# The next-to-last expert of a mixture also finishes its own rows on chip

## The chip, the cores and the metric

The kernel runs on one core of one Trainium2 chip. The metric is the device time of one launch in microseconds (us): the median of several runs. The profile is of one execution; its times count from the start of its span.

## The reference

One encoder layer over 2048 tokens of 1024 features: neighbourhood attention and a spatial gating unit share an input and an output projection, a layer norm follows, and then a mixture of experts with a second layer norm. The change touches only the mixture. Each token picks one of 4 groups of experts, and two of the 4 experts in it:

```python
def hierarchical_moe(h, w_rg, b_rg, w_re, b_re, w_gate, w_up, w_down):
    ...
    y = jnp.zeros_like(hf)
    for e in range(MOE_EXPERTS):
        act = jax.nn.silu(hf @ w_gate[e]) * (hf @ w_up[e])
        y = y + combine[:, e:e + 1] * (act @ w_down[e])
    return y.reshape(B, T, D)
...
x = layer_norm(DEEPNORM_ALPHA * x + moe_out, ln2_g[l], ln2_b[l])
```

`combine` is zero but for a token's two experts. The kernel divides the last line by ALPHA: it adds the weighted expert outputs to the first norm's result and normalizes that with a suitably smaller epsilon.

## The kernel before, in words

Routing sorts the tokens. `table` holds a list of rows for each expert (token number to gather, token number to add to, weight), `gtok` one for each group. The first norm's result lies in DRAM twice: `x1d`, which experts gather from, and `xad`, to which their outputs are added.

The experts are worked through as 18 jobs (`JOBS`, lines 36 and 37), ordered so that the four experts of a group follow each other and the largest come first. A job has up to 384 rows in parts of at most 128; jobs 14 to 17 are the last group's four experts, job 16 has two parts of 128 rows, job 17 parts of 128 and 64. In `main` (line 1313) the loop of line 1626 goes over the jobs j, and in it u = 0 to 3 counts four units. In unit u TensorE (PE) multiplies a quarter of job j's gate and up weights (`gate_up`, line 1164). Beside that, the unit issues work for neighbouring jobs: `listed` (1121) loads job j+2's list, `gather` (1135) fetches its rows into one of four buffers `xg`, `flip` (1144) transposes job j+1's rows, `load_gu` and `load_d` (1069, 1099) load weights by SyncE's (SP's) DMA queue, and `down` (1227) multiplies a part of job j-1 by its down weights, scales it on ScalarE (ACT) into a tile `y`, and adds that to `xad` with an indirect DMA of GpSimd (POOL), `add_rows` (1253). Most products are split into high and low halves, three matmuls each; job 17 (`G32`, `D32`) uses plain fp32.

When a group's last job has been added, its tokens are finished in tiles of 128 (`GTILES`: 6, 5, 5, 3). `records` (1539) loads the group's list. `combine` (1488) is a generator that goes one step further in each unit: it fetches a tile from `xad`, lets three units pass (`WAIT`), then issues the statistics and the first instruction of the norm, in the next unit the second, in the next the place, an indirect DMA to `out`. `CU` and `CT` say in which units a new tile joins: `CT` = (0, 2) in jobs 15 to 17. A tile's norm costs VectorE (DVE) `bn_stats` twice and `bn_aggr`, POOL two small instructions (line 1453 and the power in `inv`, 1456), and DVE two instructions over 128x1024, `first` (1461) and `second` (1464):

```python
        def combine(g, rec):
            x = fetch(g, rec)
            for _ in range(WAIT):
                yield
            yield from norm(x)
            place(x, rec)
            yield pipe
```

The last group is finished by `last` (1509), which follows a string, `TAIL` (63). Its tiles 0 to 2 come from the group's list; its tiles 3 and 4 are job 17's own two parts. Those rows' sum before job 17 is fetched into the `xg` buffers that the gathered rows have left, and job 17's output is added on chip, by DVE from PSUM. The letters are: f fetch, d down product and addition, s statistics on DVE, a statistics on ACT (`act_stats`, 1496), c `first`, v `second`, o place. The fetches are issued in unit 2 of job 17, everything else after its unit 3. Tokens of job 17 stand in the group's list too, so their place ("fin") waits until the places of tiles 0 to 2 ("out") have landed.

PE, ACT, DVE and POOL take their instructions in the order in which the program issues them; nothing reorders them. `apart` (1239) says which DMAs on `xad` must wait for which: a fetch of a group waits for the adds of the group's latest job.

Of the kernel before, what the change touches and what calls it, by code (L numbers as in the profile page):

```python
# [8 lines left out]
F32 = mybir.dt.float32  # L9
# [3 lines left out]
OP = mybir.AluOpType  # L13
# [45 lines left out]
D32 = (17,)  # L59
DN = 0, 0  # L60
TU = 3
CT = (0, 2)
TAIL = "f0 f3 f1 f4 f2", "s0 c0 d3 a1 v0 d4 o0 c1 a2 v1 o1 c2 a3 v2 o2 a4 c3 v3 o3 c4 v4 o4"
AW1 = 3
# [947 lines left out]
class Moe:  # L1012
    def __init__(self, c, w_gate, w_up, w_down, ln2g, ln2b, out):
        self.c, self.es = c, ExitStack()
        self.w = w_gate, w_up, w_down
        self.ln2g, self.ln2b, self.out = ln2g, ln2b, out
        self.gw, self.dw, self.ex = {}, {}, []
        self.xt, self.act, self.idx, self.added = {}, {}, {}, [[], [], [], []]
        self.parts, self.slot, n = [], [], 0
        for _, lo, hi in JOBS:  # L1020
            self.parts.append([min(P, hi - lo - o) for o in range(0, hi - lo, P)])
            self.slot.append(n)
            n += len(self.parts[-1])
# [97 lines left out]
    def listed(self, j):  # L1121
# [10 lines left out]
        if m:  # L1132
            nc.sync.dma_start(t[0:m, n], c.table[bass.ds(base + (lo + n * P), m), :])

# [78 lines left out]
    def products(self, j, s):  # L1213
        ah, al = self.acts[2 * (j % 2):2 * (j % 2) + 2]
        o = slice(s * P, s * P + self.parts[j][s])
        for n in range(2):
            po = self.bank("gu" if j in D32 else "yp")[0:self.parts[j][s], :]
# [9 lines left out]
    def down(self, j, s):  # L1227
        c, tc, nc = self.c, self.c.tc, self.c.nc
        m = self.parts[j][s]
        y = self.sp.tile([P, D], F32, name="y")  # L1230
        w = self.idx[j][0:m, s, 2:3].bitcast(F32)
# [4 lines left out]
        tc.add_to_no_dep_group(f"add{j}", r.ins)  # L1236
        self.apart(r, JOBS[j][0] // 4, j)

    def apart(self, r, g, add=None):
# [73 lines left out]
    def main(self):  # L1313
# [160 lines left out]
        def fetch(g, rec, x=None):  # L1474
# [3 lines left out]
                                         bounds_check=T, oob_is_err=False)  # L1478
            self.apart(r, g)
            return x  # L1480

# [26 lines left out]

        def last(n):
            j = nj - 1  # L1510
            x = [None] * n + [xg[(self.slot[j] + s) % NXG][0:m, :] for s, m in enumerate(self.parts[j])]
            rows = [recs[3][:, i] for i in range(n)] + [self.idx[j][0:m, s] for s, m in enumerate(self.parts[j])]
            z, mean, r, sums = {}, {}, {}, {}
            for ops in TAIL:
                for op, i in ((o[0], int(o[1])) for o in ops.split()):
                    if op == "f":
                        x[i] = z[i] = fetch(3, rows[i], x[i])
                    elif op == "d":
                        su = sums[i] = small(x[i], "csu", 5)
                        for h, po in self.products(j, i - n):  # L1520
                            hs = slice(h * 512, (h + 1) * 512)
                            V.scalar_tensor_tensor(x[i][:, hs], po, rows[i][:, 2:3].bitcast(F32), x[i][:, hs],
                                                   op0=OP.mult, op1=OP.add, accum_out=su[:, 3 + h:4 + h])
                        z[i] = xp.tile([P, D], F32, name="y")[0:self.parts[j][i - n], :]
                    elif op == "s":
                        m, r[i] = stats(x[i])
                        mean[i] = m, OP.subtract
                    elif op == "a":
                        m, r[i] = act_stats(x[i], sums.get(i))
                        mean[i] = m, OP.add  # L1530
                    elif op == "c":
                        first(z[i], x[i], *mean[i])
                    elif op == "v":
                        second(z[i], r[i])
                    elif op == "o":
                        place(z[i], rows[i], out, "out" if i < n else "fin")
                yield

# [82 lines left out]
        nj = len(JOBS)  # L1621
        todo, recs = [], {}
        junk = pl.tile([P, D], F32, name="junk")
        self.load_d(pipe, 2, 0, LAG)
        self.load_gu(pipe, 3, 0, LAG)
        for j in range(2, nj):
# [4 lines left out]
            for u in range(4):  # L1631
# [20 lines left out]
                if f < 2 and jn < nj:  # L1652
                    self.load_d(pipe, jn, f, LAG)
                if j in LASTS and u == 2:
                    recs[LASTS[j]] = records(LASTS[j])
                if j < nj - 1 and j - 1 in LASTS and u == (TU if j == nj - 4 else 3):
                    todo += [(LASTS[j - 1], i) for i in range(GTILES[LASTS[j - 1]])]
                pipe.step()
                if todo and u in (CU if j < nj - 3 else CT):
                    g, i = todo.pop(0)  # L1660
                    pipe.add(combine(g, recs[g][:, i]))
                if j == nj - 1 and u >= 2:
                    if u == 2:
                        tail = last(GTILES[3])
                    else:
                        pipe.flush()
                        assert not todo
                    next(tail)
        for _ in tail:
            pass  # L1670
        rare()
# [76 lines left out]
```

## Time and profile before

| | us |
|---|---|
| median of 3 runs (lowest, highest) | 1306.78 (1304.14, 1308.53) |
| the profiled execution, its own time | 1304.38 |
| its span in the profile | 1302.7 |
| PE busy | 1229.2 |
| DVE busy | 763.6 |
| ACT busy | 569.1 |
| POOL busy | 404.3 |

In a timeline a row is an instruction, or several alike in a row: start and duration in us, the engine, the line of the kernel, the operation, the tiles written and read (`cx` is a tile being finished, `xg` a gathered part, `crec` and `ix` are lists, `cr` and `csu` small numbers of a norm), shapes, how many, and in brackets how long the engine stood idle before it and what ended that. SPq is the DMA queue of SP. A DMA's row is its issue, not its transfer.

### The profile page before, as it was taken

What the parts mean: (1) busy time and instruction counts of PE and PEld (TensorE: products, weight loads), DVE (VectorE), ACT (ScalarE), POOL (GpSimd) and SP (SyncE); (2) the same over time, 40 slices, a digit from 0 to 9 for tenths busy, and PEclk for the clock granted to TensorE, in tenths of its full rate; (3) what the DMA queues carried; (4) which work ended last, traced back from release to release, by engine and by line L of the source; (5) the groups of instructions that cost most, each with busy time, mean ns of one, the idle gap of its engine ahead of it and who ended that gap; (6) DMA issues with size and microseconds to landing.
All of it is one profiled execution on the core that took longest, in us unless ns stands there. A gap on an engine that the chain in (4) does not pass through costs nothing. (4 is left out here: it accounts for less than half of the span.)

```text
span 1302.7 us, 22220 instructions
## 1 busy us (share of the span) xinstructions
PE 1229.2 (94%) x7948; PEld 1048.2 (80%) x7948; DVE 763.6 (59%) x1647; ACT 569.1 (44%) x1202; POOL 404.3 (31%) x416
## 2 busy tenths in 40 slices
PE   9999999999999898999999999988898999999980
PEld 7888888888888687888888888768787899989970
DVE  5366233426733226675675776866466578778665
ACT  5243142323331247554454545334556555655522
POOL 0011000001100013333534434432223357566575
PEclk9999999999999898999999999999899999999995
DMA  8514434541257669678578676362999899999984
GB/s 258 186 49 162 162 129 164 183 171 33 98 186 239 201 204 271 179 210 195 141 210 193 156 210 193 112 216 83 252 285 294 247 275 322 301 271 317 301 243 136
DMA packets 136161, 261.72 MB, mean 201 GB/s; under 512 B 51120, under 2 KB 60592, under 8 KB 136048
## 3 DMA queue, kind: packets, MB, share of 16 engines
q1 hardware_dynamic: 118064, 204.88, 50.0%
q0 software_dynamic: 17984, 55.40, 15.6%
q8 instruction: 63, 1.03, 0.3%
q14 instruction: 50, 0.41, 0.1%
HBM read 184.17 MB, written 80.24 MB: 203 GB/s over the span
## 5 line engine op out<-in xcount | busy, mean ns | idle before, releaser
L142 DVE TENSOR_TENSOR wl<-wr,wh 128x512 fp32r<-128x512 f32 (+1 forms) x132 | 125.5, 963 | 112.4 <-ACT wh L141 101.4
L653 POOL TENSOR_SCALAR lg<-lg,s 128x352 f32<-128x352 f32 (+3 forms) x128 | 79.6, 622 | 291.2 <-DVE s L652 231.9
L141 ACT CAST wh<-wr 128x512 fp32r<-128x512 f32 (+1 forms) x132 | 109.0, 839 | 87.7 <-DMA wr<-w_in 37.3
L131 PE MATMUL acc<-wh,xh 128*128 128x512 f32 x320 | 125.8, 393 | 0.4 <-ACT wh L141 0.4
L133 PE MATMUL acc<-wh,xl 128*128 128x512 f32 x320 | 124.7, 390 | 0.0
L132 PE MATMUL acc<-wl,xh 128*128 128x512 f32 x320 | 124.7, 390 | 0.0
L131 PE MATMUL gu<-xh,wh 128*128 128x256 f32 (+2 forms) x416 | 124.0, 298 | 0.0
L133 PE MATMUL gu<-xh,wl 128*128 128x256 f32 (+2 forms) x416 | 123.6, 297 | 0.0
L132 PE MATMUL gu<-xl,wh 128*128 128x256 f32 (+2 forms) x416 | 123.5, 297 | 0.0
L668 ACT COPY pT<-pt 128x384 f32<-128x384 f32 (+3 forms) x128 | 57.5, 449 | 109.9 <-PE pt L666 109.1
L131 PE MATMUL acc<-xh,wh 128*128 128x512 f32 x256 | 100.4, 392 | 0.0
L133 PE MATMUL acc<-xh,wl 128*128 128x512 f32 x256 | 99.7, 389 | 0.0
L132 PE MATMUL acc<-xl,wh 128*128 128x512 f32 x256 | 99.6, 389 | 0.0
L640 DVE CUSTOM_DVE_ANT_0 lg<-l,tm 128x352 f32<-128x352 f32 (+3 forms) x128 | 57.8, 452 | 69.2 <-PE l L133 55.8
L271 POOL TENSOR_TENSOR r<-va,mhalf 128x32 f32<-128x32 f32 x4 | 22.4, 5612 | 229.2 <-DVE va L269 229.2
L1254 POOL DMA_INDIRECT xad<-y,ix x38 | 64.1, 1687 | 68.1 <-ACT y L1233 46.7
L131 PEld LDWEIGHTS gu<-xh,wh 128*128 128x128 f32 x416 | 78.8, 190 | 1.4
L132 PEld LDWEIGHTS gu<-xl,wh 128*128 128x128 f32 x416 | 78.7, 189 | 1.2
L133 PEld LDWEIGHTS gu<-xh,wl 128*128 128x128 f32 x416 | 78.7, 189 | 0.0
L1139 POOL DMA_INDIRECT xg<-x1d,ix x40 | 48.0, 1201 | 82.8 <-DMA ix<-table 50.4
L133 PEld LDWEIGHTS acc<-wh,xl 128*128 128x128 f32 x320 | 60.1, 188 | 12.9 <-DVE xl L142 0.3
L131 PEld LDWEIGHTS acc<-wh,xh 128*128 128x128 f32 x320 | 60.2, 188 | 12.7 <-ACT wh L141 0.7
(327 smaller groups left out, 3179.7 us busy)
## 6 DMA issues: line engine op xcount, KB each, us to landing
wr<-w_in SPq DMA_DIRECT2D x72, 256.0 KB
wr<-w_down SPq DMA_DIRECT2D x34, 512.0 KB
kt<-kd SPq DMA_DIRECT2D x24, 704.0 KB
wr<-w_gate SPq DMA_DIRECT2D x30, 512.0 KB
wr<-w_up SPq DMA_DIRECT2D x30, 512.0 KB
sd<-kt SPq DMA_DIRECT2D x16, 512.0 KB
qb<-qd SPq DMA_DIRECT2D x64, 128.0 KB
sr<-sd SPq DMA_DIRECT2D x16, 512.0 KB
```

What stands on the lines that cost most here:

```text
L131: nc.tensor.matmul(out, lhsT=ahi, rhs=bhi, start=first, stop=False)
L132: nc.tensor.matmul(out, lhsT=ahi, rhs=blo, start=False, stop=False)
L133: nc.tensor.matmul(out, lhsT=alo, rhs=bhi, start=False, stop=last)
L141: nc.scalar.copy(hi, src)
L142: nc.vector.tensor_tensor(lo, src, hi.bitcast(F32), op=OP.subtract)
L271: nc.gpsimd.tensor_tensor(r, va, mhalf[:, :, :], op=OP.pow)
L640: nc.vector.tensor_tensor_reduce(out=l[:, :N], in0=o.rearrange("p r c -> p (r c)"), in1=bias, scale=-1.0, scalar=3.0e38, op0=OP.add, op1=O ...
L653: nc.gpsimd.tensor_scalar(l[:, :N], l[:, :N], s, 1.0, op0=OP.mult, op1=OP.mult)
L668: nc.scalar.copy(w[0:n, 0:len(ch)], pt[0:n, 0:len(ch)])
L1139: nc.gpsimd.indirect_dma_start(out=self.xg[(self.slot[j] + s) % NXG][0:m, :], out_offset=None, in_=c.x1d[0:rows, :], in_offset=bass.Indire ...
L1254: return self.c.nc.gpsimd.indirect_dma_start(out=self.c.xad[0:rows, :], out_offset=bass.IndirectOffsetOnAxis(ap=ix, axis=0), in_=y, in_off ...
```

## The change

Job 16's parts become the tiles 5 and 6 of `last`. In unit 3 of job 16 five fetches are issued: tiles 0 to 2, and job 16's own rows (5, 6), before job 16's output is in `xad`. The letter e is new: it adds job 16's `y` to its tile on chip. Job 16's output is still added to `xad`, because job 17's rows and the others need it; those two adds now wait for the five fetches (`reads`). `DN` moves job 16's two down products from unit 0 of job 17 to unit 1. Tiles 0 to 2 are finished in the units of job 17; in its unit 3 tiles 3 and 4 are fetched and tiles 5 and 6 finished; behind the loop `ENDS` finishes tiles 3 and 4. Places are now in three classes, "out", "pen" and "fin", each after the one before.

The last group's list is loaded in unit 2 of job 15 rather than job 16. `CT` lets the five tiles of the group before join in units 0 to 3 of job 15 (the first joins in unit 3 of job 14, as before); a tile's fetch is issued in the unit after it joins. So these five are fetched in units 0, 1, 2, 3 of job 15 and 0 of job 16, where it was 0, 1, 3 of job 15 and 1, 3 of job 16.

For job 17's 64-row part the two halves of the output go to partitions 0 to 63 and 64 to 127 of one PSUM bank, and their matmuls alternate between the two column groups of PE. The part's list is loaded twice, so that the weights lie on both halves of the partitions.

```diff
-DN = 0, 0
+DN = 1, 1
-CT = (0, 2)
-TAIL = "f0 f3 f1 f4 f2", "s0 c0 d3 a1 v0 d4 o0 c1 a2 v1 o1 c2 a3 v2 o2 a4 c3 v3 o3 c4 v4 o4"
+CT = (0, 1, 2, 3), (), ()
+TAIL = {(16, 3): "f0 f1 f2 f5 f6", (17, 0): "s0 c0", (17, 1): "v0 o0 s1 c1", (17, 2): "v1 o1 a2 c2 v2 o2",
+        (17, 3): "f3 f4 e5 a5 e6 a6 c5 v5 o5 c6 v6 o6"}
+ENDS = "d3 a3 d4 a4 c3 v3 o3 c4 v4 o4"
+HALF = 64
...
         if m:
-            nc.sync.dma_start(t[0:m, n], c.table[bass.ds(base + (lo + n * P), m), :])
+            for o in (0, HALF) if j in D32 else (0,):
+                nc.sync.dma_start(t[o:o + m, n], c.table[bass.ds(base + (lo + n * P), m), :])
...
+        if j in D32 and self.parts[j][s] == HALF:
+            po = self.bank("gu")
+            for k in range(2):
+                for n in range(2):
+                    self.c.nc.tensor.matmul(po[n * HALF:(n + 1) * HALF, :], lhsT=self.act[j, k][:, o],
+                                            rhs=self.dw[j, k][0][:, n * 512:(n + 1) * 512], start=k == 0, stop=k == 1)
+            for n in range(2):
+                yield n, po[n * HALF:(n + 1) * HALF, :]
+            return
...
         self.apart(r, JOBS[j][0] // 4, j)
+        info = mybir.DependencyInfo(mybir.DependencyClass.Sync, mybir.DependencyReason.DATA)
+        for name in self.reads if j == len(JOBS) - 2 else ():
+            tc.add_manual_dep(r.ins, name, info, reason="read first")
...
             self.apart(r, g)
+            if rec is not None and g == 3:
+                self.reads.append(r.ins.name)
...
+        def last(ops):
+            if ops and not fin:
+                fin.update({i: (None, None, None, recs[3][:, i]) for i in range(GTILES[3])})
+                fin.update(enumerate(own(nj - 1) + own(nj - 2), GTILES[3]))
...
+                elif op == "e":
+                    V.tensor_tensor(x, x, self.ys[j, k][0:x.shape[0], :], op=OP.add)
...
+                elif op == "o":
+                    place(z[i], row, out, {None: "out", nj - 2: "pen", nj - 1: "fin"}[j])
...
-                if j in LASTS and u == 2:
+                if j in LASTS and u == 2 and j < nj - 2:
                     recs[LASTS[j]] = records(LASTS[j])
+                if j == nj - 3 and u == 2:
+                    recs[3] = records(3)
...
-                if todo and u in (CU if j < nj - 3 else CT):
+                if todo and u in (CU if j < nj - 3 else CT[j - nj + 3]):
                     g, i = todo.pop(0)
                     pipe.add(combine(g, recs[g][:, i]))
-                if j == nj - 1 and u >= 2:
-                    if u == 2:
-                        tail = last(GTILES[3])
-                    else:
-                        pipe.flush()
-                        assert not todo
-                    next(tail)
-        for _ in tail:
-            pass
+                if j == nj - 1 and u == 3:
+                    pipe.flush()
+                    assert not todo
+                last(TAIL.get((j, u), ""))
+        last(ENDS)
```

## Rows read from the trace of the kernel before

**Rows 1.** The page: each engine's busy time, share of the span, instructions.

```profile
PE 1229.2 (94%) x7948; PEld 1048.2 (80%) x7948; DVE 763.6 (59%) x1647; ACT 569.1 (44%) x1202; POOL 404.3 (31%) x416
```

**Rows 2.** Busy times by stretch: PE, PEld, DVE, ACT, POOL, TensorE clock, DMA share, GB/s.

```profile
1280.00:1290.00 10.00, 0.00 (x0) 0.00 (x0) 7.72 (x7) 4.85 (x13) 8.80 (x10) 0.50 0.26 104
```

**Rows 3.** Timeline of DVE, jobs 16 and 17: start, duration, instruction, idle before.

```profile
1229.32 1.28 DVE L1450 BATCH_NORM_STATS2 cst<-cx 128x6 f32<-128x512 f32 x2 [2.56 <-DMA cx<-xad,crec]
...
1236.68 1.29 DVE L1450 BATCH_NORM_STATS2 cst<-cx 128x6 f32<-128x512 f32 x2 [1.64 <-DMA cx<-xad,crec]
...
1240.59 0.42 DVE L1207 TENSOR_TENSOR sg<-gu,sg 128x256 f32<-128x256 f32 x1
...
1241.83 1.28 DVE L1465 SCALAR_TENSOR_TENSOR cx<-cx,cr,l2b 128x1024 f32<-128x1024 f32 x1
1244.13 1.23 DVE L142 TENSOR_TENSOR dl<-wr,dh 128x1024 fp32r<-128x1024 f32 x1 [1.02 <-ACT dh L141]
...
1256.63 1.29 DVE L1450 BATCH_NORM_STATS2 cst<-cx 128x6 f32<-128x512 f32 x2 [5.25 <-DMA cx<-xad,crec]
...
1261.41 1.28 DVE L1450 BATCH_NORM_STATS2 cst<-cx 128x6 f32<-128x512 f32 x2
...
1262.97 1.28 DVE L1462 SCALAR_TENSOR_TENSOR cx<-cx,cmv,l2g 128x1024 f32<-128x1024 f32 x1
```

**Rows 4.** Timeline of POOL, from job 16 to the tail's five reads.

```profile
1246.68 1.04 POOL L1476 DMA_INDIRECT cx<-xad,crec  x1 [0.30 <-issue]
...
1253.64 1.60 POOL L1254 DMA_INDIRECT xad<-y,ix  x1 [1.30 <-ACT y L1233]
1255.55 1.58 POOL L1254 DMA_INDIRECT xad<-y,ix  x1 [0.30 <-issue]
...
1265.30 1.94 POOL L1476 DMA_INDIRECT cx<-xad,crec  x1 [0.35 <-issue]
...
1270.17 0.96 POOL L1476 DMA_INDIRECT xg<-xad,ix  x1 [0.30 <-issue]
1271.44 1.01 POOL L1476 DMA_INDIRECT cx<-xad,crec  x1 [0.30 <-issue]
```

**Rows 5.** Timeline of DVE in the tail.

```profile
1270.49 1.29 DVE L1450 BATCH_NORM_STATS2 cst<-cx 128x6 f32<-128x512 f32 x2 [4.22 <-DMA cx<-xad,crec]
...
1277.24 0.74 DVE L1522 SCALAR_TENSOR_TENSOR xg<-gu,ix,xg 64x512 f32<-64x512 f32 x1 [0.80 <-DMA xg<-xad,ix]
...
1284.22 1.28 DVE L1465 SCALAR_TENSOR_TENSOR cx<-cx,cr,l2b 128x1024 f32<-128x1024 f32 x1 [0.74 <-POOL cr L1458]
1285.43 1.28 DVE L1462 SCALAR_TENSOR_TENSOR y<-xg,csu,l2g 128x1024 f32<-128x1024 f32 x1
1287.43 1.28 DVE L1465 SCALAR_TENSOR_TENSOR y<-y,cr,l2b 128x1024 f32<-128x1024 f32 x1 [0.73 <-POOL cr L1458]
...
1290.63 1.28 DVE L1465 SCALAR_TENSOR_TENSOR y<-y,cr,l2b 64x1024 f32<-64x1024 f32 x1 [0.73 <-POOL cr L1458]
```

**Rows 6.** Timeline of POOL at the end.

```profile
1286.51 0.24 POOL L1506 TENSOR_SCALAR csu<-csu 128x1 f32<-128x1 f32 x1
...
1287.63 2.02 POOL L1483 DMA_INDIRECT out<-cx,crec  x1 [0.23 <-issue]
...
1294.49 0.93 POOL L1483 DMA_INDIRECT out<-y,ix  x1 [0.30 <-POOLq L1549]
```

**Rows 7.** Timeline of SP's queue: the last group's list.

```profile
1244.36 0.33 SPq L1544 DMA_DIRECT2D crec<-gtok  x1
```

**Rows 8.** Timeline of ACT in the tail: two tiles' sums.

```profile
1276.31 1.06 ACT L1500 ACTIVATE junk<-cx 128x1024 f32<-128x1024 f32 x1 [16.72 <-DMA cx<-xad,crec]
...
1279.00 1.06 ACT L1500 ACTIVATE junk<-cx 128x1024 f32<-128x1024 f32 x1
```

**Rows 9.** Timeline of PE: job 16's and job 17's down products.

```profile
1248.94 0.50 PE L131 MATMUL yp<-dh,a 128*128 128x512 f32 x1 [1.98 <-ACT a L141]
...
1264.58 8.12 PE L1222 MATMUL gu<-dh,sg 128*128 128x512 f32 x14 [1.90 <-DVE sg L1207]
```

More of the change, by code (lines that the diff above doesn't have):

```diff
@@ L1018, in __init__ @@
         self.xt, self.act, self.idx, self.added = {}, {}, {}, [[], [], [], []]
+        self.ys, self.reads = {}, []
         self.parts, self.slot, n = [], [], 0
@@ L1229, in down @@
         m = self.parts[j][s]
-        y = self.sp.tile([P, D], F32, name="y")
+        y = self.ys[j, s] = self.sp.tile([P, D], F32, name="y")
         w = self.idx[j][0:m, s, 2:3].bitcast(F32)
@@ L1507, in act_stats @@
             return su[:, 1:2], inv(su[:, 2:3])
[L1509 to L1537, printed above, removed]
@@ new lines, in own @@
+        def own(j):
+            return [(j, s, xg[(self.slot[j] + s) % NXG][0:m, :], self.idx[j][0:m, s])
+                    for s, m in enumerate(self.parts[j])]
+        def last(ops):
+            if ops and not fin:
+                fin.update({i: (None, None, None, recs[3][:, i]) for i in range(GTILES[3])})
+                fin.update(enumerate(own(nj - 1) + own(nj - 2), GTILES[3]))
+            for op, i in ((o[0], int(o[1])) for o in ops.split()):
+                j, k, x, row = fin[i]
+                if op == "f":
+                    x = fetch(3, row, x)
+                    fin[i], z[i] = (j, k, x, row), x
+                elif op == "d":
+                    su = sums[i] = small(x, "csu", 5)
+                    for h, po in self.products(j, k):
+                        hs = slice(h * 512, (h + 1) * 512)
+                        o = HALF * h if x.shape[0] == HALF else 0
+                        w = self.idx[j][o:o + x.shape[0], k, 2:3].bitcast(F32)
+                        V.scalar_tensor_tensor(x[:, hs], po, w, x[:, hs], op0=OP.mult, op1=OP.add,
+                                               accum_out=su[:, 3 + h:4 + h])
+                    z[i] = xp.tile([P, D], F32, name="y")[0:x.shape[0], :]
+                elif op == "e":
+                    V.tensor_tensor(x, x, self.ys[j, k][0:x.shape[0], :], op=OP.add)
+                elif op == "s":
+                    m, rstd[i] = stats(x)
+                    mean[i] = m, OP.subtract
+                elif op == "a":
+                    m, rstd[i] = act_stats(x, sums.get(i))
+                    mean[i] = m, OP.add
+                elif op == "c":
+                    first(z[i], x, *mean[i])
+                elif op == "v":
+                    second(z[i], rstd[i])
+                elif op == "o":
+                    place(z[i], row, out, {None: "out", nj - 2: "pen", nj - 1: "fin"}[j])
@@ L1622, in main @@
         todo, recs = [], {}
+        fin, z, mean, rstd, sums = {}, {}, {}, {}, {}
         junk = pl.tile([P, D], F32, name="junk")
```

## The prediction

> **What bounds the kernel now.** I read the page first: TensorE (PE) is busy for 94% of the span, so a microsecond is saved either on PE or behind its last matmul [rows 1]. Next I read the busy times by stretch: from 1280 to 1290 us PE does nothing, VectorE (DVE) is busy for 7.72 of 10 us and GpSimd (POOL) for 8.80, and TensorE is granted 0.50, its 1.2 GHz level [rows 2]. The change moves work in this tail and just ahead of it. The chain of waits has only the last write in it, so I followed the tail by hand in the timelines of DVE and POOL, two engines that take their instructions in the order of the program.
>
> DVE first [rows 3]. While PE works on job 16, DVE waits for rows that finishing tiles of the group before (I call them c0 to c4) have fetched: 2.56 us for c0, 1.64 for c1, 5.25 for c3. So it runs late: c4's statistics, called for in unit 2 of job 17, start at 1261.41. Then POOL [rows 4]: the reads of the last group's three tiles and of job 17's two own parts (f0, f3, f1, f4, f2) stand behind c4's two small POOL instructions and begin at 1265.30. f0's rows are there at 1270.49, when DVE starts on them, f4's at 1277.24 [rows 5]. From then on the tail is a tempo: one tile's second instruction follows the other's after 3.21 us (1284.22, 1287.43, 1290.63), because each waits for two small POOL instructions. It ends with the write issued at 1294.49, over at 1295.42, and 7.28 us follow it to the end of the span [rows 6].
>
> **The change, part by part.** I call the issue of f0 X, and ask where X goes and how long the way is from X to the end. Before it is 1302.7 - 1265.30 = 37.4 us.
>
> *Spacing of c1 to c4 and the earlier list.* c2, c3 and c4 are now read in units 2 and 3 of job 15 and unit 0 of job 16, so c3's 5.25 us wait has no cause any more. X comes behind c4's small instructions in unit 3 of job 16. DVE must do all that stands ahead of it. I start at c1's second instruction, 1241.83, which depends only on reads issued as before. An instruction over a 128x1024 tile takes 1.2 us from start to start (1284.22 to 1285.43), statistics 1.56 (1261.41 to 1262.97), the product of gate and up with its split 1.24 (1240.59 to 1241.83), the split of w_down 1.2 (its row has 1.23) [rows 3, 5]. Up to c4's first instruction there are three statistics (4.68), six tile instructions (c1's second, c2's and c3's both, the split: 7.2) and one product (1.24): 13.1 us. I add 1.0 us for c2's second instruction, whose POOL instructions stand behind an add and a place. c4's first is then at 1255.9. Before it took 2.33 us from there to f0 (1262.97 to 1265.30), so X = 1258.3: **7.0 us earlier**. c4's rows are due at 1254.4. The slowest such read took 9.95 us, from 1246.68 to 1256.63; c4's now stands ahead of that place by an add (1.91) and a place (1.3), so near 1243.5, and lands by 1253.4 [rows 3, 4]. That cover is 1 us; what is missing of it would be added to X. The list itself moves ahead of weight loads on SP: one issue of 0.33 us [rows 7], and the doubled 64 index rows are another. SP issued the list at 1244.36, and PE came to job 17's last products only at 1264.58 [rows 7, 9], so I cost both at nothing; the ends are 0 and 0.7 us.
>
> *Two more tiles.* f0, f1, f2, f5 and f6 go out together. By before's pattern f0's rows are at DVE at X + 5.19 = 1263.5 and the fifth read is issued at X + 6.14 = 1264.4 [rows 4, 5].
>
> *The wait that the change adds.* Job 16's two adds now wait until all five reads have landed, since the tiles of job 16's own rows must not see them. Before shows no such wait, so I bound the landing of the fifth read. Low: f0 took 5.19 us, of which POOL spent 0.97 beyond a normal read's issue (1.94 against 0.97 for f4), so 4.2 us: 1268.6. High: f4, fourth of five, took 7.07 us (1270.17 to 1277.24): 1271.5 [rows 4, 5]. I take the high end, because f6 is the fifth of five full reads in one queue. What is queued behind the adds on POOL is the point: c4's place, tile 0's place and tile 1's two small instructions, and DVE needs the latter for v1, tile 1's second instruction. Adds follow each other after 1.91 us, reads and places after 1.3 (1270.17 to 1271.44), the small ones take 0.9 [rows 4, 6]: 1271.5 + 2 x 1.91 + 2 x 1.3 + 0.9 = 1278.8 for v1. DVE could have had it at 1263.5 + 2 x 1.56 + 3 x 1.2 + 0.4 + 0.5 (one wait for POOL) = 1271.1. **DVE waits 7.7 us here.**
>
> The Trainium skill's page "DMA: Bandwidth & Descriptors", section "Anatomy of one DMA — SWDGE (gpsimd) path", gives a lone transfer about 2.0 us plus its bytes by 436 GB/s; for half a megabyte that is an estimated 3.2 us, f6 would be in at 1267.6, and the sum would be the second rival's. The trace does not agree for reads that follow each other: f4, half as large, took 7.07 us.
>
> *From v1 to the end.* v2 comes 3.2 us on, at 1282.0. Behind it on DVE stand job 17's last product (0.4) and the two new additions of job 16's y (1.2 each; the first over at 1284.8). ScalarE's statistics of tile 5 take 2.69 us (1276.31 to 1279.00 [rows 8]), POOL 0.9: v5 at 1288.4, v6 at 1291.6. Then job 17's two parts: 1.2 us to the first product-and-add, 1.35 each for both (the row's two halves of 0.74), 1.2 to v3, at 1296.7, and v4 at 1299.9. v4 takes 1.28, the write's issue another 0.94 (1287.63 + 2.02 against the end of its v), and 7.28 follow: **1309.4, or 6.7 us later than 1302.7** [rows 5, 6]. Of X's gain of 7.0 us nothing is left, because the way from X grew from 37.4 to 51.1 us.
>
> *PE.* Job 16's down products move behind the next unit; that fills PE's wait of 1.98 us for their activations [rows 9]. It pays nothing: job 17's last product stands behind v2 on DVE and PE waits for that.
>
> *Column groups.* The matmuls of the last products start at 1283.6. 16 of them by 0.58 (8.12 us for 14 [rows 9]) are over at 1292.9, while DVE wants the 64-row part at 1294.1: hidden with or without pairs. Were each twice as long, at the low clock all through, with pairs they would end at 1297.5, 3.4 us late; that is the upper end.
>
> The sum is against the profiled execution: 1304.38 us, 1.7 us beyond its span and 2.4 below the median of 1306.78. With 6.7 on top that execution would be 1311.1 and the median 1313.5. Its own range: -2.9 if the reads land at the low end, -1 and +1.5 on X, +3.4 for the matmuls: 1309 to 1318. A measurement of this kernel tells apart about 0.3%, 3.9 us.
>
> **The rivals.**
> *DVE's own work sets the end (faster).* The place is v1, and the mechanism that the reads and POOL's small instructions are always there before DVE asks. From f0's rows at 1263.5 DVE's instructions alone are two statistics (3.1), ten tile instructions (c0, v0, c1, v1, c2, v2, c5, v5, c6, v6: 12.0), two products (0.8), two additions (2.4), the parts' product-and-adds (2.7) and c3, v3, c4 (3.6): v4 starts at 1288.1, and with 1.28, 0.94 and 7.28 the span ends at 1297.6, 5.1 us under before; median 1301.7. My sum has 11.8 us of DVE's waits on top; it is faster by over 0.3% only from where they are under 1.2 us together. For it: three tiles have left the end of the program, and DVE waited under 0.8 us at each second instruction in the tail [rows 5]. Against it: POOL's order puts two adds that wait for reads ahead of v1. Chance 0.22.
>
> *The hold is short (no change).* The reads land by 1268.6 or sooner, and the rest goes as in my sum. POOL has f6's issue, c3's place and tile 0's small instructions to do until 1268.0 anyway (1264.4 + 2 x 1.3 + 0.9), so the end is 2.9 to 3.5 us sooner, 1305.9 to 1306.5, at most 3.8 over before; median 1310.3. For it: no weights are in flight any more at 1258, as they were not for f0, which took 4.2 us; against it f4's 7.07. Chance 0.28.
>
> *The catch-up fails.* c1's or c4's rows come later, as the reads go out closer together among the weights; X stays at 1262 or later and the end moves to 1313, median 1317. I count it into the forecast's side, 0.12 of its 0.50.
>
> *The change does not do what it says:* the column groups may run one after the other. That changes no end here, since those matmuls are covered.
>
> **How the numbers follow.** The forecast is the likeliest case: 1313.5. It and the failed catch-up have 0.50, nearly all of it slower by over 0.3%. The short hold has 0.28, within 0.3%, and the fast case 0.22, faster by over 0.3%. The range goes down past the fast case by 1.7 us, for what a median of runs may stand off, to 1300.0, and up to the upper end, 1318.
>
> **What would show it.** Right: f0 issued near 1258; POOL's adds of job 16 waiting for a read, until about 1271; DVE idle for several us ahead of v1; PE waiting over 15 us for job 17's last product; a DVE tempo of 3.2 us up to the end. Wrong: f0 before 1250, or adds that start right behind the small instructions, or a DVE without gaps from f0's rows on; then one of the first two rivals is at work.

## The result and the profile after

The changed kernel is slower: 1318.00 us in the median of 5 runs (1317.68 to 1320.01), against 1308.53 us (1304.14 to 1309.22, 5 runs) for the kernel before in the same comparison; ratio 1.0088, 95% interval 1.0063 to 1.0113 (the two medians alone differ by 9.5 us, 0.72%). The prediction was 1313.5 us. The profiled execution took 1317.68 us, its span is 1316.0.

The two profiled spans differ by 13.3 us, but not all of that is the change. The last instruction that both kernels do alike is PE's transposition of job 17's 64-row part (line 1158 before, 1163 after). It starts at 1234.22 us before and at 1236.41 after: 2.19 us of the difference arise ahead of it, in code that is the same in both. From this **mark** to the end it is 68.5 us before and 79.6 after, so the change itself costs **11.1 us** in these two profiles, where 6.7 were predicted. Below I compare kernels by their time behind the mark. This measure scatters: eight kernels of this study (the changed one, order, dn0, nogroups, ahead, noown, reads, small) are alike up to the issue of f0, and there f0 comes 23.4 to 25.7 us behind the mark. So a difference of 2 us behind the mark tells nothing by itself. The time from f0 to the end leaves that scatter out (55.4 us in the changed kernel, 55.4 in nogroups; 37.4 before) and is given beside it. Each such figure is from one profiled execution.

The page's busy times answer to [rows 1]:

```profile
PE 1228.6 (93%) x7948; PEld 1047.5 (80%) x7948; DVE 771.6 (59%) x1656; ACT 571.0 (43%) x1207; POOL 415.4 (32%) x424
```

PE's busy time is the same within 0.6 us, DVE's is 8.0 us longer, POOL's 11.1. One stretch of the tail in the busy times by stretch (columns as in [rows 2]):

```profile
1270.00:1280.00 10.00, 0.00 (x0) 0.00 (x0) 3.97 (x5) 2.59 (x5) 5.22 (x5) 0.60 0.64 170
```

From 1270 to 1280 DVE works for only 3.97 of 10 us: the new hole. TensorE has no work and is granted 0.60, most of the stretch at its 1.2 GHz level, as in the tail before [rows 2]. The timeline of DVE shows the hole and what follows it; the rows answer to [rows 3, 5] (statistics of c3 and of tile 0, then v1, v2, v5, v6, the first of the four parts of d3 and d4, v3, v4):

```profile
1251.45 1.28 DVE L1467 BATCH_NORM_STATS2 cst<-cx 128x6 f32<-128x512 f32 x2
...
1265.61 1.29 DVE L1467 BATCH_NORM_STATS2 cst<-cx 128x6 f32<-128x512 f32 x2 [4.12 <-DMA cx<-xad,crec]
...
1281.31 1.28 DVE L1482 SCALAR_TENSOR_TENSOR cx<-cx,cr,l2b 128x1024 f32<-128x1024 f32 x1 [6.98 <-POOL cr L1475]
...
1285.64 1.28 DVE L1482 SCALAR_TENSOR_TENSOR cx<-cx,cr,l2b 128x1024 f32<-128x1024 f32 x1 [1.85 <-POOL cr L1475]
...
1293.13 1.28 DVE L1482 SCALAR_TENSOR_TENSOR xg<-xg,cr,l2b 128x1024 f32<-128x1024 f32 x1 [0.73 <-POOL cr L1475]
...
1296.05 1.29 DVE L1482 SCALAR_TENSOR_TENSOR xg<-xg,cr,l2b 128x1024 f32<-128x1024 f32 x1 [0.44 <-POOL cr L1475]
1297.25 0.75 DVE L1547 SCALAR_TENSOR_TENSOR xg<-gu,ix,xg 128x512 f32<-128x512 f32 x1
...
1302.16 1.29 DVE L1482 SCALAR_TENSOR_TENSOR y<-y,cr,l2b 128x1024 f32<-128x1024 f32 x1 [0.74 <-POOL cr L1475]
...
1305.08 1.28 DVE L1482 SCALAR_TENSOR_TENSOR y<-y,cr,l2b 64x1024 f32<-64x1024 f32 x1 [0.44 <-POOL cr L1475]
```

c3's wait of 5.25 us is gone, f0's rows come 4.9 us earlier on the clock (7.1 us by the mark), and then DVE waits 6.98 us at v1. POOL's timeline says for what; the rows answer to [rows 4, 6] (f0, the fifth read f6, the first add, tile 1's second small instruction, o1, o2, f3, tile 5's first small instruction, the last two places):

```profile
1260.56 1.91 POOL L1493 DMA_INDIRECT cx<-xad,crec  x1 [0.38 <-issue]
...
1266.67 0.99 POOL L1493 DMA_INDIRECT xg<-xad,ix  x1 [0.30 <-issue]
...
1274.12 1.74 POOL L1271 DMA_INDIRECT xad<-y,ix  x1 [3.86 <-DMA xg<-xad,ix]
...
1280.71 0.57 POOL L1475 TENSOR_TENSOR cr<-cmv,mhalf 128x1 f32<-128x1 f32 x1
1282.89 1.82 POOL L1502 DMA_INDIRECT out<-cx,crec  x1 [1.61 <-DVE cx L1482]
...
1287.22 2.03 POOL L1502 DMA_INDIRECT out<-cx,crec  x1 [1.61 <-DVE sg L1212]
1289.55 1.03 POOL L1493 DMA_INDIRECT xg<-xad,ix  x1 [0.30 <-PE gu L1236]
...
1291.92 0.52 POOL L1525 TENSOR_SCALAR csu<-csu 128x1 f32<-128x1 f32 x1
...
1305.23 2.06 POOL L1502 DMA_INDIRECT out<-y,ix  x1 [0.19 <-issue]
1307.60 0.93 POOL L1502 DMA_INDIRECT out<-y,ix  x1 [0.30 <-POOLq L1575]
```

The first add waits 3.86 us for the last of the five reads; the places and the small instructions that DVE needs stand behind the adds. Read on: o1 waits for v1 and goes out only at 1282.89, o2 for v2 at 1287.22, and f3 and f4, the reads of job 17's own rows, stand behind o2. f3, issued 26.4 us ahead of the end, is a row to remember. PE's last products, answering to [rows 9]:

```profile
1255.12 0.79 PE L134 MATMUL yp<-dh,a 128*128 128x512 f32 x1 [3.37 <-ACT a L144]
...
1287.25 5.47 PE L1236 MATMUL gu<-dh,sg 128*128 128x512 f32 x6 [17.34 <-DVE sg L1212]
1292.65 1.94 PE L1225 MATMUL gu<-dh,sg 128*64 128x512 f32 x8
```

PE waits 17.34 us for job 17's activations, which DVE computes behind v2. The last row is the 64-row part in column groups: eight matmuls in 1.94 us.

### The profile page after: what moved, and what is told of

Read it like the earlier page. It is cut to its first block, busy times and chain, and to the rows that moved or that the text cites. A ratio compares the mean times of both kernels' runs of the same rounds, so it can differ in the third digit from the quotient of the medians.

```text
span 1316.0 us, 22253 instructions
## 1 busy us (share of the span) xinstructions
PE 1228.6 (93%) x7948; PEld 1047.5 (80%) x7948; DVE 771.6 (59%) x1656; ACT 571.0 (43%) x1207; POOL 415.4 (32%) x424
## 5 line engine op out<-in xcount | busy, mean ns | idle before, releaser
L135 PEld LDWEIGHTS acc<-wl,xh 128*128 128x128 f32 x320 | 60.1, 188 | 12.7 <-DVE wl L145 0.7
```

What stands on the lines that cost most here:

```text
L135: nc.tensor.matmul(out, lhsT=ahi, rhs=blo, start=False, stop=False)
```

## The experiments

The question is what the 11.1 us are made of. I started from the prediction's own theory: the adds that wait for the reads hold back what stands behind them on POOL, so an order that puts less behind them should give most of the loss back. The first runs take parts of the change away (dn0, nogroups, spacing) or mend that order (order). From their misses grew a second theory: the tail now goes twice through memory in a row, reads before adds and adds before the reads f3 and f4, and this would set the end whatever the order. The later runs set the two against each other; each expectation states its theories for itself.

### order

Tile 1's statistics and first instruction and tile 2's statistics (on ACT) are issued ahead of job 16's adds.

```diff
-(17, 0): "s0 c0", (17, 1): "v0 o0 s1 c1", (17, 2): "v1 o1 a2 c2 v2 o2"
+(17, 0): "s0 c0 s1 c1 a2", (17, 1): "v0 o0", (17, 2): "v1 o1 c2 v2 o2"
```

> The changed kernel, but tile 1's statistics and tile 2's are issued in unit 0 of job 17, so that their four small POOL instructions stand ahead of job 16's two adds instead of behind them. Theory (the adds wait for the five reads, and what is queued behind them on POOL is what DVE waits for): the 7 us wait of DVE ahead of tile 1's second instruction goes, v1 comes right behind c1, f3 and f4 go out about 6 us sooner, and the end is 5 to 7 us earlier than the changed kernel's: about 1312 us against 1318. Rival (two more tiles are simply more work for DVE and POOL): the waits turn up elsewhere, the end moves by less than 2 us.

Measured: 1317.95 us (1315.66 to 1321.33, 6 runs), ratio 1.0087 (1.007 to 1.0104), no gain in the time, where 5 to 7 us were expected; 78.8 us behind the mark against 79.6, and 53.1 from f0 against 55.4. In DVE's timeline the wait at v1 is gone (v0 and v1 stand in one row), and another has come, 6.56 us at job 17's last product:

```profile
1277.47 2.47 DVE L1482 SCALAR_TENSOR_TENSOR cx<-cx,cr,l2b 128x1024 f32<-128x1024 f32 x2
...
1289.43 0.36 DVE L1212 TENSOR_TENSOR sg<-gu,sg 128x192 f32<-128x192 f32 x1 [6.56 <-PE gu L1204]
```

ACT's and PE's timelines tell why:

```profile
1276.12 1.06 ACT L1519 ACTIVATE junk<-cx 128x1024 f32<-128x1024 f32 x1 [14.89 <-DMA cx<-xad,crec]
...
1278.68 1.25 ACT L1247 ACTIVATE y<-yp,ix 128x512 f32<-128x512 f32 x2
...
1279.40 0.79 PE L134 MATMUL yp<-dh,a 128*128 128x512 f32 x1 [14.14 <-ACT y L1247]
```

Tile 2's statistics (`a2`) wait for its rows on ACT, and the scaling of job 16's `y`, without which PE's banks don't come free, now stands behind them; PE waits 14.14 us for it. The second add goes out at 1285.12. The hold was not removed; it went to ACT and PE, which also take their instructions in order.

### dn0

Job 16's down products back in unit 0 of job 17, all else as in the changed kernel.

```diff
-DN = 1, 1
+DN = 0, 0
```

> The changed kernel with job 16's down products and adds back in unit 0 of job 17 (DN = 0, 0). Theory (queue behind the adds): the reads land no sooner, so now tile 0's small instructions stand behind the waiting adds as well; v0 moves from 1270 to about 1280, v1 to about 1285, the end is some 4 us later than the changed kernel's, about 1322 us. Rival (it is the later down products on PE that cost): as fast as before or at least 3 us faster than the changed kernel.

Measured: 1320.96 us (1320.25 to 1322.39, 4 runs), ratio 1.011 (1.0091 to 1.0129); 82.9 us behind the mark, 3.3 more than the changed kernel, and 58.1 from f0, 2.6 more (about 4 was expected; the intervals of the two ratios overlap, so this rests on the profiles). The adds now stand ahead of tile 0's small instructions and wait 5.77 us for the same reads; DVE's wait moves from v1 to v0 and grows to 10.46 us:

```profile
1281.18 1.28 DVE L1482 SCALAR_TENSOR_TENSOR cx<-cx,cr,l2b 128x1024 f32<-128x1024 f32 x1 [10.46 <-POOL cr L1475]
```

So moving the products is a part of the change that works against its loss: what stands behind the waiting adds on POOL sets the price of the wait.

### nogroups

No column groups and no second copy of the list.

```diff
-            for o in (0, HALF) if j in D32 else (0,):
+            for o in (0,):
...
-        if j in D32 and self.parts[j][s] == HALF:
+        if False:
...
-                        o = HALF * h if x.shape[0] == HALF else 0
+                        o = 0
```

> The changed kernel without the two column groups and without the second copy of the 64-row list. Theory: PE takes about 2 us longer for the last eight matmuls but DVE comes to them later still, so the time stays within 1.5 us of the changed kernel's, 1317 to 1320. Rival (the column groups pay at the end): about 2 us slower.

Measured: 1320.80 us (1312.64 to 1321.40, 4 runs), ratio 1.0092 (1.0062 to 1.0122), not to be told from the changed kernel; from f0 to the end both take 55.4 us. In PE's timeline all the products are one row:

```profile
1290.27 9.05 PE L1236 MATMUL gu<-dh,sg 128*128 128x512 f32 x14 [17.36 <-DVE sg L1212]
```

They end 9.05 us after their start, in the changed kernel 7.34 (1287.25 to 1294.59). DVE comes to the 64-row part at 1301.61, 2.3 us after PE is done, so nothing waits: from v1 to v4 it is 23.57 us, and 23.77 with column groups. The groups do what they say and are worth nothing here.

### spacing

The kernel before with the closer spacing of c1 to c4 and the early list alone.

```diff
-CT = (0, 2)
+CT = (0, 1, 2, 3), (), ()
...
-                if j in LASTS and u == 2:
+                if j in LASTS and u == 2 and j < nj - 2:
...
+                if j == nj - 3 and u == 2:
+                    recs[3] = records(3)
...
-                if todo and u in (CU if j < nj - 3 else CT):
+                if todo and u in (CU if j < nj - 3 else CT[j - nj + 3]):
```

> The kernel before with only the spacing of the five tiles (one in each unit of job 15) and the earlier list; its tail, its down products and its adds are as before. Theory: c3's wait of 5 us goes, but f0 still stands behind job 16's adds and two places on POOL, so it is issued 0.7 to 3 us sooner and the end moves by as much: 1305 to 1308 us, within 0.3% of before. Rival (the spacing alone is the loss, its reads disturb the weight loads): slower than before by 4 us or more. Rival (the spacing carries all of X's gain): 6 to 7 us faster.

Measured: 1308.97 us (1305.49 to 1313.07, 12 runs) against 1306.88 (17 runs), ratio 1.0014 (0.9998 to 1.0029): no gain, a miss. POOL's timeline (job 16's adds, then f0):

```profile
1258.17 2.51 POOL L1254 DMA_INDIRECT xad<-y,ix  x1 [0.31 <-issue]
1261.04 1.56 POOL L1254 DMA_INDIRECT xad<-y,ix  x1 [0.36 <-ACT y L1233]
...
1269.31 1.04 POOL L1476 DMA_INDIRECT cx<-xad,crec  x1 [4.07 <-issue]
```

DVE does c2 to c4 sooner, and with that job 16's last product of gate and up later (1251.89, before 1248.03), without which its down products can't start; so the adds go out at 1258.17 and 1261.04 instead of 1253.64 and 1255.55 [rows 4], and f0, which in this kernel must wait for the adds, goes out 4.0 us later than before instead of 7 earlier. The row says "issue" for its 4.07 us; I take them for the wait until the adds have landed, which the kernel asks of f0. POOL has only two places in between, over at 1265.23, and from the end of the second add's issue (1262.60) to f0 it is 6.7 us. Here, where the reads follow the adds, catching up on DVE was worth nothing.

### ahead

As order, but tile 2's statistics on DVE, so that ACT is free for `y`.

```diff
-(17, 0): "s0 c0 s1 c1 a2"
+(17, 0): "s0 c0 s1 c1 s2"
```

> As the run 'order', but tile 2's statistics are taken on DVE instead of ScalarE, so that nothing on ScalarE stands ahead of job 16's scaled products; all six small POOL instructions of tiles 0 to 2 stand ahead of the two adds. Theory (the hold reaches the end through what is queued behind the adds; in 'order' the hold only moved to ScalarE and from there to PE): DVE runs from f0's rows to v2 without a wait of over 2 us, v2 comes about 7 us sooner against job 17's last flip than in the changed kernel, PE no longer waits 14 us, and the time is 5 to 7 us below the changed kernel's, about 1312 us, still above before. Rival (the added work on DVE and POOL sets the end): within 2 us of the changed kernel, 1316 to 1320.

Measured: 1314.51 us (1312.30 to 1318.81, 6 runs), ratio 1.0059 (1.0040 to 1.0078); 75.3 us behind the mark, 4.3 less than the changed kernel, and 51.5 from f0, 3.9 less; a little under the 5 to 7 expected. (The intervals of the two ratios overlap, so this too rests on the profiles.) DVE works from f0's rows to v2 without a data wait, and then:

```profile
1275.23 1.28 DVE L1482 SCALAR_TENSOR_TENSOR cx<-cx,cr,l2b 128x1024 f32<-128x1024 f32 x1
...
1287.60 1.28 DVE L1482 SCALAR_TENSOR_TENSOR xg<-xg,cr,l2b 128x1024 f32<-128x1024 f32 x1 [5.68 <-POOL cr L1475]
```

v5 waits 5.68 us. On POOL the adds, four places and f3, f4 stand ahead of tile 5's small instructions. Neither the adds nor f3 wait for a transfer any more: the adds stand directly behind tile 2's small instructions, f3 behind the fourth place:

```profile
1273.32 2.13 POOL L1271 DMA_INDIRECT xad<-y,ix  x1 [0.18 <-issue]
1275.76 2.21 POOL L1271 DMA_INDIRECT xad<-y,ix  x1 [0.30 <-issue]
...
1284.35 1.03 POOL L1493 DMA_INDIRECT xg<-xad,ix  x1 [0.30 <-issue]
...
1286.73 0.19 POOL L1525 TENSOR_SCALAR csu<-csu 128x1 f32<-128x1 f32 x1
```

f3 is 26.3 us ahead of the end (1310.6), as in the changed kernel. The same distance shows in order (26.4), dn0 (26.4), nogroups (26.2) and ahead2 (26.3): in these kernels whatever was done ahead of f3 only moved f3.

### ahead2

As ahead, with job 16's own rows fetched one unit earlier, in unit 2 of job 16.

```diff
-(16, 3): "f0 f1 f2 f5 f6"
+(16, 2): "f5 f6", (16, 3): "f0 f1 f2"
```

> 'ahead' with the two reads of job 16's own rows one unit earlier, so that only three reads are in flight behind tile 2's. Theory: the adds are released 3 us sooner, f3 and f4 go out 3 us sooner, and as these set the end once v1 does not, the time falls by another 2 to 4 us, to about 1309 us. Rival (DVE sets the end by then): no change against 'ahead'.

Measured: 1316.04 us (1313.70 to 1319.76, 6 runs), ratio 1.0064 (1.0046 to 1.0081), 77.7 us behind the mark and 51.7 from f0, where ahead has 51.5: no gain, a miss. f5 goes out at 1257.72, only 6 us ahead of f0 (1263.60): on POOL it stands behind c3's small instructions, over at 1255.76, then waits another 1.95 us (its row names PE), and the two reads hold up c4's small instructions (c4's second instruction waits 3.14 us on DVE). The expectation had overlooked that in ahead the adds no longer waited for a read; here too, at 1278.03, they stand directly behind tile 2's small instructions.

### noown

Tiles 5 and 6 are left out: job 16's own rows are not finished unless they are job 17's too, so this kernel leaves out part of the output and only shows what these tiles cost.

```diff
-(16, 3): "f0 f1 f2 f5 f6"
+(16, 3): "f0 f1 f2"
...
-(17, 3): "f3 f4 e5 a5 e6 a6 c5 v5 o5 c6 v6 o6"
+(17, 3): "f3 f4"
```

> The changed kernel without tiles 5 and 6: the rows of job 16 that are not also job 17's are left unfinished; three reads are waited for instead of five. Theory: the adds go out 3.5 us sooner and v1 with them, and DVE, ScalarE and POOL lose the tiles' 5 to 7 us between v2 and job 17's first product-and-add; together 8 to 10 us below the changed kernel, about 1309 us, so about as before. Rival (the spacing, the down products' place or the early tiles are the loss): still 5 us or more above before.

Measured: 1310.06 us (1306.42 to 1313.72, 10 runs), ratio 1.003 (1.0014 to 1.0045). Behind the mark 71.7 us, 7.9 less than the changed kernel (8 to 10 were expected) and still 3.2 more than before, though two tiles of work are missing; from f0 48.3 us, 7.1 less than the changed kernel. With three reads instead of five the first add goes out 9.7 us after f0 (1257.10 to 1266.80; 13.6 in the changed kernel). v1 still waits 5.00 us behind the adds, and at the end DVE waits for PE:

```profile
1274.83 1.28 DVE L1482 SCALAR_TENSOR_TENSOR cx<-cx,cr,l2b 128x1024 f32<-128x1024 f32 x1 [5.00 <-POOL cr L1475]
...
1286.85 0.75 DVE L1547 SCALAR_TENSOR_TENSOR xg<-gu,ix,xg 128x512 f32<-128x512 f32 x1 [6.13 <-PE gu L1236]
```

PE had waited 14.27 us for the activations that DVE computes behind v2, so that wait goes back to v1 as well.

### reads

As ahead, with f3 and f4 asked for as early as POOL's queue allows, behind job 16's adds and two places.

```diff
-(17, 2): "v1 o1 c2 v2 o2",
-(17, 3): "f3 f4 e5 a5 e6 a6 c5 v5 o5 c6 v6 o6"
+(17, 2): "f3 f4 v1 o1 c2 v2 o2",
+(17, 3): "e5 a5 e6 a6 c5 v5 o5 c6 v6 o6"
```

> 'ahead' with the reads of job 17's own rows (f3, f4) directly behind tile 0's place, ahead of the places of tiles 1 and 2. Theory (two round trips through DRAM in a row set the end: five reads, then job 16's adds, then f3 and f4): f3 can go out only when the adds have landed, some 4 to 5 us behind the second add's issue, so it gains 1 to 2 us over 'ahead' and no more, and the end 0 to 2 us. Rival (POOL's places in front of f3 are what is left): f3 goes out about 3 us sooner, right behind tile 0's place, and the time falls by 3 us.

Measured: 1315.62 us (1312.17 to 1317.62, 6 runs), ratio 1.0067 (1.0043 to 1.0091), 77.6 us behind the mark, 52.9 from f0; no gain over ahead. Now the second trip is seen by itself in POOL's timeline:

```profile
1279.15 2.19 POOL L1271 DMA_INDIRECT xad<-y,ix  x1 [0.30 <-issue]
...
1286.70 1.04 POOL L1493 DMA_INDIRECT xg<-xad,ix  x1 [2.08 <-DMA xad<-y,ix]
...
1291.71 0.19 POOL L1525 TENSOR_SCALAR csu<-csu 128x1 f32<-128x1 f32 x1
```

f3 waits for the adds to land, 5.4 us after the end of the second add's issue (1279.15 + 2.19 = 1281.34). Asked for earlier, it only blocks POOL's queue: tile 5's small instruction comes at 1291.71, behind f4 and two more places, and DVE waits 7.29 us at v5. Those two places are also why f3 is 28.7 us ahead of the end here.

### places

The kernel before with tile 0's place moved up in its string, ahead of other work on POOL.

```diff
-"s0 c0 d3 a1 v0 d4 o0 c1 a2 v1 o1 c2 a3 v2 o2 a4 c3 v3 o3 c4 v4 o4"
+"s0 c0 d3 v0 o0 a1 d4 c1 a2 v1 o1 c2 a3 v2 o2 a4 c3 v3 o3 c4 v4 o4"
```

> The kernel before with one letter group moved in its tail: tile 0's place goes out ahead of tile 1's two small POOL instructions instead of behind them. Theory (in the tail, DVE's second instructions wait for POOL, and a place that stands ahead of the next tile's small instructions sets the 3.2 us from tile to tile): the first place fills a gap of POOL, v2 and the later tiles come about 1 us sooner, and the end 1 to 3 us: a gain under 0.3%, at 1304 to 1306 us where the kernel before has 1306.6. Rival (ScalarE's statistics, 2.7 us a tile, set the tempo): no change.

Measured: 1306.72 us (1303.09 to 1308.65, 12 runs) against 1306.02, ratio 0.9999 (0.9983 to 1.0015): a miss. From f0 to the end it is 36.4 us (37.4 before), a microsecond that the runs can't tell; of the tempo one interval became shorter, 2.93 us between tile 1's and tile 2's second instructions, and the next was 3.21 again.

### small

As ahead, with the small instructions of tiles 5 and 6 ahead of f3 and f4 and the places spread between them. It takes away the wait at v5 that ahead left, and was meant to decide between the two theories, A (serial trips) and B (order).

```diff
-(17, 1): "v0 o0", (17, 2): "v1 o1 c2 v2 o2",
-(17, 3): "f3 f4 e5 a5 e6 a6 c5 v5 o5 c6 v6 o6"
+(17, 1): "v0", (17, 2): "v1 c2 v2 o0",
+(17, 3): "e5 a5 o1 e6 a6 f3 f4 o2 c5 v5 c6 v6 o5 o6"
```

> The order of 'ahead', and in unit 3 of job 17 the small instructions of job 16's own tiles stand ahead of the fetches f3 and f4, and the places of tiles 0 to 2 are spread between them. All times by the mark of the 64-row flip, against 'ahead' (75.3 us from the mark to the end). Both theories: the 5.68 us wait at v5 goes, v5 comes 5 us earlier. Theory A (two round trips in a row, reads - adds - reads, set the end): f3 cannot be issued before the adds have landed, about 5.4 us behind the second add's issue, so it stays within 1.5 us of where it was (49 us behind the mark), its rows come 5 us after that, d3 on VectorE now waits for them and is at most 2.5 us earlier; end 73 to 75 us behind the mark, median 1311 to 1314. Theory B (GpSimd's queue order at v5 is all that is left of the loss): the 5 us carry through to the end, 70 us behind the mark, median about 1309, equal to before within 0.3%.

Measured: 1318.97 us (1317.76 to 1319.61, 4 runs), ratio 1.0088 (1.0056 to 1.0121); 77.1 us behind the mark (its mark is at 1239.88), 1.8 more than ahead where A expected 0.3 to 2.3 less and B about 5; from f0 52.9, 1.3 more than ahead. DVE's timeline (v5, d3):

```profile
1287.64 1.28 DVE L1482 SCALAR_TENSOR_TENSOR xg<-xg,cr,l2b 128x1024 f32<-128x1024 f32 x1 [0.74 <-POOL cr L1475]
...
1297.17 0.75 DVE L1547 SCALAR_TENSOR_TENSOR xg<-gu,ix,xg 128x512 f32<-128x512 f32 x1 [5.03 <-DMA xg<-xad,ix]
```

The wait at v5 fell from 5.68 to 0.74 us, and 5.03 us of waiting for f3's rows came at d3. POOL's timeline shows the second add, tile 6's second small instruction and f3:

```profile
1280.73 2.21 POOL L1271 DMA_INDIRECT xad<-y,ix  x1 [0.30 <-issue]
...
1290.25 0.57 POOL L1475 TENSOR_TENSOR cr<-csu,mhalf 128x1 f32<-128x1 f32 x1
1291.10 2.00 POOL L1493 DMA_INDIRECT xg<-xad,ix  x1 [0.29 <-issue]
```

f3 goes out 51.2 us behind the mark (49.0 in ahead), 25.9 us ahead of the end. The 5 us did not carry through to the end, so B falls as it was stated; that the end came even later than A had it is a miss of A's number. But A is not shown either: with the 5.4 us of reads the adds would have landed near 1288.3, and f3 goes 2.8 us later, directly behind tile 6's small instructions. It is POOL's order, not the adds, that held f3 here. As an estimate, 2.8 us less would leave the end 74.3 us behind the mark, still 5.8 later than before. Of the 1.8 us over ahead, 0.8 arise ahead of d3 and 1.1 behind it: the places o5 and o6 now stand ahead of tile 3's small instructions on POOL, o5 goes only 4.26 us after o2 has been issued, and v3 waits 1.85 us for the small ones.

## Why the prediction came out as it did

Times of the changed kernel that stand beside a predicted one have the 2.19 us of the mark taken off, to stand on the clock of the profile before; pairs of times (from, to) are as in the rows.

**Spacing and X: right.** f0 at 1258.4 (predicted 1258.3), its rows at DVE at 1263.4 (1263.5), the fifth read at 1264.5 (1264.4). That it agrees to 0.1 us is luck, as f0 scatters by 2.3 us behind the mark; the way there (c1's second instruction at 1242.2 for 1241.8, c4's first at 1256.0 for 1255.9) was right. The cover of c4's rows held: DVE starts on c2, c3 and c4 without a wait for their rows. What the prediction did not say is that the gain needs the reads to be free of the adds; spacing shows it, where the same catch-up by itself moved f0 later.

**The wait that the change adds: right.** The first add goes at 1271.9 (1271.5), so the high bound was the one to take; v1 comes at 1279.1 (1278.8) after a wait of 6.98 us (7.7). The add goes 7.45 us after the issue of the fifth read (1266.67 to 1274.12). The figure of a lone transfer that the prediction took from the Trainium skill's page "DMA: Bandwidth & Descriptors", section "Anatomy of one DMA — SWDGE (gpsimd) path" (an estimated 3.2 us for half a megabyte), does not hold for the last of five reads in one queue: 7.45 us were measured.

**From v1 to the end: this is the step that failed.** It was "v2 comes 3.2 us on", then DVE's durations one after another: 30.6 us from v1 to the span's end. Measured are 34.7 (1281.31 to 1316.0). Term by term, as lateness against the prediction: v1 0.3 us, v2 1.5 (1283.5 for 1282.0), v5 2.5 (1290.9 for 1288.4), v6 2.3, v3 3.3 (1300.0 for 1296.7), v4 3.0 (1302.9 for 1299.9), issue of the last place 4.2 (1305.4 for 1301.2), end 4.4 (1313.8 for 1309.4). So "a DVE tempo of 3.2 us up to the end", one of the signs named for being right, did not come: v2 follows v1 after 4.33 us, v6 follows v5 and v4 follows v3 after 2.92. At three of these terms (v2, v5, the last place) a transfer on POOL that I had not put into the sequence is what grew. o1 cannot go until v1 is done, and tile 2's small instructions stand behind it, so v2 is 4.33 us behind v1, not 3.2. o2, f3 and f4 stand ahead of tile 5's small instructions (1287.22 to 1291.92). From v6 to v3 the missing 1.0 us is mostly v3's wait of 0.74 us for its small instructions, which I had left out. At the end the 128-row place, issued for 2.06 us, stands ahead of the 64-row one, which goes at 1307.60, not right after v4. The prediction said that everything behind a waiting instruction counts, and then carried on from v1 with a tempo read in a tail that had no reads and no waiting places between its tiles [rows 5]. It had read these 3.21 us as a wait for POOL, though only 0.73 of each are waiting and the rest is DVE's own two instructions.

The measured 1318.00 us is also the upper end of the stated range, but by another way: that end was made of job 17's matmuls taking twice as long. They stayed hidden, and the 4.4 us came mostly from POOL's queue.

**PE: the payoff right, a detail wrong.** PE waited 17.34 us for job 17's last product (over 15 was predicted). But its wait of 1.98 us for job 16's activations [rows 9] was not filled; it grew to 3.37, at no cost to the end. **Column groups: right**, hidden with or without (nogroups).

**The rivals.** "DVE's own work sets the end" is out: DVE waits 6.98 us at v1, and in the kernels where that wait is taken away (order, ahead, small) another of 5.0 to 6.6 us takes its place. "The hold is short" is out by the first add's time. "The catch-up fails" did not happen.

**What the loss is.** The changed kernel gains 6.9 us at f0 (24.2 us behind the mark instead of 31.1, with the scatter named above) and pays 18.0 from f0 to the end (55.4 us for 37.4). noown, with 48.3 us from f0, says that 7.1 of the 18.0 belong to tiles 5 and 6 and their reads. Part of the rest is the way through memory. Before, one dependence of this kind stood ahead of the tail, adds, then the five reads, and other work covered it: the second add's issue was over at 1257.13 and f0 went at 1265.30 [rows 4]. Now there are two in a row: reads, then adds (13.6 us from f0 to the first add), and adds, then the reads f3 and f4. `reads` shows the second by itself, and `small` that d3 waits for f3's rows once v5 does not wait. As an estimate from rows: 13.6 us to the first add, 3.6 for both issues (1274.12 to 1277.75), 5.4 for the landing (reads), 5.1 from f3 to its rows (f0's, 1260.56 to 1265.61; 6.1 in small), 18.7 from d3 to the end (1297.25 to 1316.0, the same in ahead: 1291.87 to 1310.6) make 46.4 us from f0, when 44.3 (37.4 + 6.9) would only equal the kernel before. Even with no other hold ahead of d3 this arrangement would come out about 2 us slower than before; by the rows of reads, whose adds go 14.2 us after f0 and take 4.6, about 4. That is little more than f0's scatter of 2.3 us. No kernel that does the whole work reached this bound: ahead needs 51.5 us from f0. So by this estimate the serial trips hold 2 to 4 of the 11.1 us, and the other 7 to 9 lie in the engines' queues: the work of tiles 5 and 6, and what stands in front of what. Of these the orders tried got back 3.9 at most (ahead). That no order can win is estimated, not shown; what is shown is that none of these did.

What stays open: the wait of the adds for the reads was not taken away by itself, since the adds would then change rows being read; its price is known only through noown, which takes work away with it. That f3 is some 26 us ahead of the end in so many kernels has two causes of the same length: in the changed kernel and ahead the small instructions behind f3 and f4, in small f3's rows. And where the 2.19 us ahead of the mark come from was not followed up; the mark lies between 1233.7 and 1240.8 us in the profiles of this study, in code that is the same. It tends to lie later where the granted clock, averaged over the span, is lower (0.975 before, 0.973 after, 0.968 in order), so the clock is the likely cause, not shown. No version here beats the kernel before.

## What to carry to other kernels

Before moving reads ahead of an accumulating write, count the serial dependences through memory to the end, before and after: a tail that went write, then read, and now goes read, write, read has one more landing on its path, and none of the orders tried here got back more than a part of what it cost. When kernels are compared by a mark in their traces, see first how far the same code scatters behind that mark. When a wait enters an engine that works in order, write out that engine's whole queue from there to the end with every transfer in it, and don't carry on with a tempo measured where the queue held other things. Moving the waiting work to another in-order engine moves the wait with it.

## What the runs showed of the hardware

- An accumulating add lands late: a read that waits for it could start only 5.4 us after the end of its issue, 7.6 after the start (reads, the second of two adds, 1279.15 to 1286.70); in spacing it was 6.7 us after the end, where the row names no releaser. A first read's rows were in use 5.1 us after the start of its issue (changed kernel, 1260.56 to 1265.61).
- The issue of an indirect read or place on POOL takes about 1.0 us. Where it starts beside a DVE instruction over 128x1024 with two tile operands it took up to 2.1 us and ended 0.9 to 1.0 us behind that instruction: f0 at 1260.56 took 1.91 us, beside DVE's 1.28 us from 1260.21, c3's place at 1267.97 took 1.39, beside DVE's 1.29 from 1267.18, and the read after f0, with DVE idle, 1.00. DVE's own 1.28 us did not change.
- Two column groups do run together: in order, both at a granted clock of 1.00, eight matmuls for 128 rows took 3.60 us (the row at 1289.16; the next begin at 1292.69) and eight in column groups 1.94. The whole of these products took 9.05 us without column groups (nogroups) and 7.34 with them (changed kernel), both granted 0.50 at their start.
